# One layer's S5 in-chunk products moved ahead in the step order, their skewed table on two queues, output weights in whole rows

## The chip, the cores and the metric

The kernel runs on one core of a Trainium2 chip. The core has five engines that run side by side, each with an instruction stream of its own: TensorE (PE, matrix products; PEld is its weight load), VectorE (DVE), ScalarE (ACT), GpSimd (POOL) and SyncE (SP), which here only issues transfers. Transfers run on 16 DMA engines. The metric is the device time of one execution in microseconds (us). The kernel before took 1331.38 us, the median of three runs (1319.96 to 1343.16).

## The reference

256 latent tokens and 256 context tokens of width 1024 go through two layers in float32. Layer 0 has mLSTM heads beside attention. Layer 1, which the change touches, has S5 channels beside Mamba-2 (SSD) heads, and only its latent tokens are wanted at the end. Each layer closes with a mixture of 16 experts (MoE). Layer 1's mixer, cut to what matters:

```python
u_l, z_l, xbc_l, dt_l = split(h @ w_in)                       # and the same of the context
s5l = s5_output(s5_bidir(u_c, u_l, s5p), u_l, ...)            # gelu, then g * sigmoid(g @ glu_w + glu_b)
ssl = ssd_output(ssd_bidir(...), z_l, ssd_norm)               # y * silu(z), then an RMS norm
y = concatenate([s5l, ssl]) @ w_out                           # w_out is 1024 x 1024
```

`s5_bidir` runs a complex diagonal recurrence over the tokens in both directions for 32 groups of 16 channels and 64 states: `h = A h + B u`, `y = Re(C h)`. `ssd_bidir` is the chunked form of a scan over 8 heads: a term from within a chunk (`cb * decay`) and one from the state that is carried in.

## The kernel before, in words

**The whole.** Layer 0, its MoE, layer 1, its MoE stand one behind the other. The code is written in Python on a framework that orders the instructions of PE, DVE, ACT and POOL by a simulated schedule; the transfers on SP go out in the order of the code. `self.after(x, y)` only tells that scheduler to put x behind y, and sets no semaphore. What an engine waits for on the chip is set by data and by buffers alone.

**The stage of the change** is the second half of `layer1` (from L2131). It has four generators that give out work in steps, and the string `STEPS` (L1371) sets the order in which the loop at L2139 takes steps of them: S is the SSD heads, I the S5 in-chunk table, Y the S5 output products (C, the scan, was stepped before).

- **I, `s5_intra`** (L1587). For 32 groups it computes the response of a channel to another over 8 positions back and forth, a table E of 128 x 8 x 240, by 256 small matmuls (L1610, 32 columns of weights, 16 or 112 columns of data; those with `ca` or `v` among their operands read the S5 output tables). ACT copies the result out of PSUM (L1613), DVE adds the skip term (L1615), and POOL's queue writes E to a small DRAM table `ed` in 4 transfers (L1617).
- **The skew, `s5_skew`** (L1628). The table is read back from `ed` 8 times per half, each time shifted by 16, which makes the Toeplitz form: two tiles of 128 x 4 x 4 x 128, 1 MB each, called E and LL after the buffers they take. All 16 reads are on SP (L1633). The LL buffer holds SSD's decay products until then; E's buffer is a new one.
- **Y, `s5_y`** (L1736). In a pair of PSUM banks it sums five terms: n = 0 to 3 are the output tables times the scanned state `xs` (L1755), n = 4 is the skewed table times the input U. The last 16 products per half are those that read E and LL (L1755 with `E,U` and `LL,U`).
- **S, `ssd`**. State matmuls (L1996), decay products on DVE into LL (L2019), their products with x (L2022), the carried-state products (L2034), then a norm over DVE and ACT (L2041 to L2048) and 8 transposes (L2051) into `mix`.

Behind it come the gelu, its transposes and the GLU gate (L1767 to L1806), then `out_proj1` (L2160, called through `out_proj`): 2 token tiles x 4 column chunks of 256 x 8 row blocks of w_out. `out_w1` (L2145) loads w_out by column chunks into four buffers called `v`, on SP, behind the skew: each tile is one column chunk for all eight row blocks. Rows of w_out that belong to S5 go in a permuted order, by eight 16-partition transfers a tile.

The MoE of layer 1 streams three 2 MB weights per expert on SP (L941), and its products are L981, L1288 and L1302.

Of the kernel before, what the change touches and what calls it, by code (L numbers as in the profile page):

```python
# [21 lines left out]
D = 1024  # L22
KD = 8
# [1344 lines left out]
PI = math.pi  # L1368
SEGS = 32
SCAN = 4  # L1370
STEPS = "ISIIISSSIISIIIYSYSYYSYYYYYY"  # L1371


class Odd(Moe):
# [212 lines left out]
    def s5_intra(self, tb):  # L1587


        nc, a = self.nc, self.a  # L1590
        E = self.t("E", [128, 8, 240])
        (dk, idq), sk = self.dk, self.t("sk", [128, 8, 16])
        nc.vector.tensor_mul(sk, dk[:, :, None].to_broadcast([128, 8, 16]), idq[:, None, :].to_broadcast([128, 8, 16]))
        for x in range(4):
            p = [self.ps([128, 240], "ps") for _ in range(2)]
            for part in range(2):

                for z, d, r in [(0, 0, 0), (0, 0, 1), (0, 1, 0), (0, 1, 1), (1, 0, 0), (1, 0, 1)] if part == 0 else [(1, 1, 0), (1, 1, 1)]:
                    for q in range(4):
                        for gp in range(2):  # L1600
                            h, gh = slice(gp * 64, gp * 64 + 64), 4 * x + q
                            o, b = p[gp][32 * q:32 * q + 32], ((r * 2 + d) * 16 + gh) * 16

                            if z == 0:
                                o, rhs = o[:, 112:128], self.ct[h, r, d, gh, :]
                            elif d == 0:
                                o, rhs = o[:, 128:240], tb[0][r][h, gh, 0:7, :]
                            else:
                                o, rhs = o[:, 0:112], tb[1][r][h, gh, 0:7, :][:, ::-1, :]
                            self.lastI = nc.tensor.matmul(o, self.bf[h, b:b + 32], rhs, start=(r == 0 and (d == 0 or z == 1)), stop=(r == 1 and (d == 1 or z == 1)))  # L1610
                if part:
                    for gp in range(2):
                        nc.scalar.copy(E[:, gp * 4 + x, :], p[gp])  # L1613
                yield
        nc.vector.tensor_add(E[:, :, 112:128], E[:, :, 112:128], sk)  # L1615
        for q in range(4):
            nc.gpsimd.dma_start(self.ed[:, :, q, :], E[32 * q:32 * q + 16])  # L1617
        tb.append(self.s5_skew())
        yield
# [8 lines left out]
    def s5_skew(self):  # L1628

        mt = [self.t(tag, [128, 4, 4, 128]) for tag in ("E", "LL")]  # L1630
        for g in range(2):
            for s in range(8):
                self.nc.sync.dma_start(mt[g][16 * s:16 * s + 16], self.ed[:, 4 * g:4 * g + 4, :, (7 - s) * 16:(7 - s) * 16 + 128])  # L1633
        return mt


# [99 lines left out]
    def s5_y(self, U, xs, tb):  # L1736


        nc = self.nc
        pg = self.pg = [self.ps(tag="a") for _ in range(2)]  # L1740
        for n in range(5):
            for x in range(4):
                for gp in range(2):
                    h = slice(gp * 64, gp * 64 + 64)
                    for q in range(4):
                        gh = 4 * x + q
                        if n == 4:
                            lhs, rhs = U[:, 16 * gp + gh, 32:64], tb[2][gp][:, x, q, :]
                        else:
                            d, r = divmod(n, 2)  # L1750
                            k0 = 0 if d else SEGS - 1
                            lhs, rhs = xs[h, d, r, k0:k0 + SEGS, gh], tb[d][r][h, gh]
                            if d:
                                rhs = rhs[:, ::-1, :]
                        self.lastY = nc.tensor.matmul(pg[gp][32 * q:32 * q + 32, x * 128:(x + 1) * 128], lhs, rhs,  # L1755
                                                      start=(n == 0 and x == 0), stop=(n == 4 and x == 3))
                        self.after(self.lastY, self.lastI)
                if x % 2:
                    yield

    def s5_gelu(self):

        nc, pg = self.nc, self.pg
        g2 = self.t("xsT", [128, 2, 1024])
        gl = g2[:, 0].rearrange("p (t g x c) -> p t g x c", t=8, g=2, x=4)
        for gp in range(2):
            nc.scalar.activation(gl[:, :, gp].rearrange("p t x c -> p x t c"), pg[gp].rearrange("p (x t c) -> p x t c", x=4, t=8),  # L1767
                                 AF.Gelu_apprx_tanh)
        gT = g2[:, 1].rearrange("p (q t k) -> p q t k", q=4, t=8)
        for hf in range(2):  # L1770
            p = self.ps(tag="b")
            for t in range(4):
                nc.tensor.transpose(p[:, t * 128:(t + 1) * 128], gl[:, 4 * hf + t].rearrange("p g x c -> p (g x c)"), self.ident)
            o = gT[:, :, 4 * hf:4 * hf + 4, :].rearrange("p q t k -> p t q k")
            i = p.rearrange("p (t q k) -> p t q k", t=4, q=4)
            if hf:
                nc.scalar.copy(o, i)
            else:
                nc.vector.tensor_copy(o, i)
        return gT  # L1780
# [315 lines left out]
    def layer1(self):  # L2096
        nc = self.nc
        with self.phase("O", dict(ps=3, a=2, b=2, o=1), s2=5, s4=2, nz=1, scr=1, acsb=1, m8="nz"), \
# [34 lines left out]
            with self.sub("OC", ca=2, wp=1, E=1, sk="s2"):  # L2133
# [4 lines left out]
                steps = dict(S=self.ssd(R, mixS), I=self.s5_intra(tb), Y=self.s5_y(U, xs, tb), C=scan)  # L2138
                for step in STEPS:  # L2139
                    next(steps[step], None)  # L2140
# [4 lines left out]
    def out_w1(self):  # L2145

        nc, wo = self.nc, self.a["od_w_out"][0]
        ws = []
        for c in range(4):
            w, f = self.t("v", [128, KD, 256]), slice(256 * c, 256 * c + 256)  # L2150
            for x in range(8):
                self.after(nc.sync.dma_start(w[16 * x:16 * x + 16, 0:4], wo[64 * x:64 * x + 64, f].rearrange("(q c) f -> c q f", q=4)), self.lastS)
            nc.sync.dma_start(w[:, 4:8], wo[512:1024, f].rearrange("(k p) f -> p k f", p=128))
            ws.append(w)
        return ws

    def out_proj1(self, mix, ws):
        def mm(p, i, c4):
            for k in range(KD):
                o = self.nc.tensor.matmul(p, mix[k // 4][:, k % 4, i * 128 - 256:i * 128 - 128], ws[c4][:, k, :], start=(k == 0), stop=(k == KD - 1))  # L2160
            return o
        self.out_proj(mm, 1, (2, 3), (self.lastY,))

# [38 lines left out]
```

## Time and profile before

| what | value |
|---|---|
| median of three runs | 1331.38 us |
| profiled execution | 1328.82 us |
| its span, first to last instruction | 1327.2 us |
| mean granted TensorE clock | 0.927 |
| PE busy | 1137.6 us (86%) |
| DVE busy | 605.8 us (46%) |
| ACT busy | 304.1 us (23%) |
| POOL busy | 130.0 us (10%) |
| DMA | 330.40 MB, 249 GB/s over the span |
| the stage of the change, first in-chunk matmul to first of out_proj1 | 940.4 to 1016.8 us |

Times in rows are us from the start of the span. Busy times count work, not waits. The span is cut for the rows below by stretches of the stage, since a share over the whole span mixes stages with different limits. A float32 matmul leaves two records on PE. A row of waits says which engine stood, at which line, and what it waited for last.

### The profile page before, as it was taken

Reading aid. Unit: us, or ns where it says so; the run is one execution under the profiler, and the core shown is the slowest. Engines: PE = TensorE matmul, PEld = TensorE weight load, DVE = VectorE, ACT = ScalarE, POOL = GpSimd, SP = SyncE. Lnnn points to the kernel's source line nnn. Section 1 sums busy time; section 2 is a strip of 40 time slices with the busy share of each in tenths; the row PEclk is TensorE's granted clock in tenths of the full one; section 3 lists DMA queues with packets and bytes.
Section 4 is the critical chain, followed back from the end, with each engine's and each line's share of the span. In section 5 each row is a group of like instructions: output and inputs, shape, how many; then the busy total and the mean of one; then the engine's idle time right before and its main releaser. Section 6 shows DMA issues by size and latency. Waiting matters only on the chain. (4 is left out here: it accounts for less than half of the span.)

```text
span 1327.2 us, 23457 instructions
## 1 busy us (share of the span) xinstructions
PE 1137.6 (86%) x9689; PEld 701.2 (53%) x9689; DVE 605.8 (46%) x1647; ACT 304.1 (23%) x590; POOL 130.0 (10%) x185
## 2 busy tenths in 40 slices
PE   3899998977879599999999966967867789999895
PEld 0575564656579345545665525846756643432221
DVE  2657664186247521837013188799631531211112
ACT  2425441034121111111121134346221211110000
POOL 2002020000300251212101100000000000000000
PEclk8999999999989699999999986988767889999998
DMA  7876136703993899999999742342769859999960
GB/s 275 281 269 237 50 129 223 252 2 120 320 289 123 277 309 363 348 388 352 367 337 335 280 160 66 112 112 61 289 88 199 360 203 412 420 420 420 420 256 34
DMA packets 103973, 330.40 MB, mean 249 GB/s; under 512 B 18049, under 2 KB 56089, under 8 KB 78256
## 3 DMA queue, kind: packets, MB, share of 16 engines
q1 hardware_dynamic: 94592, 298.98, 63.2%
q0 software_dynamic: 9264, 29.81, 7.1%
q8 instruction: 80, 1.31, 0.4%
q14 instruction: 37, 0.30, 0.1%
HBM read 312.68 MB, written 18.01 MB: 249 GB/s over the span
## 5 line engine op out<-in xcount | busy, mean ns | idle before, releaser
L981 PE MATMUL ps<-wa,xT 128*32 128x512 f32 x848 | 167.2, 599 | 0.0
L981 PE MATMUL ps<-wb,xT 128*32 128x512 f32 x608 | 139.3, 594 | 0.0
L87 PE MATMUL ps<-wh,hT 128*128 128x256 f32 (+2 forms) x320 | 93.9, 294 | 6.5 <-ACT wh L381 4.7
L89 PE MATMUL ps<-wh,hT 128*128 128x256 f32 (+2 forms) x320 | 93.1, 293 | 4.0 <-DVE hT L315 4.0
L153 PE MATMUL ps<-w,cT 128*32 128x512 f32 x384 | 67.7, 782 | 28.2 <-DMA w<-in_ada_w_dram 24.2
L88 PE MATMUL ps<-wl,hT 128*128 128x256 f32 (+2 forms) x288 | 83.3, 290 | 1.4 <-DVE wl L383 1.4
L984 PE MATMUL ps<-wa,xT 128*32 128x256 f32 x496 | 82.9, 381 | 0.0
L984 PE MATMUL ps<-wb,xT 128*32 128x256 f32 x480 | 82.3, 380 | 0.0
L989 ACT ACTIVATE s<-ps 64x512 f32<-64x512 f32 (+1 forms) x48 | 23.4, 516 | 247.1 <-PE ps L981 246.6
L87 PE MATMUL ps<-hT,wh 128*128 128x512 f32 (+1 forms) x160 | 61.6, 385 | 14.4 <-DVE xs L1722 11.5
L87 PEld LDWEIGHTS ps<-wh,hT 128*128 128x128 f32 x320 | 62.6, 196 | 15.2 <-issue 6.1
L89 PEld LDWEIGHTS ps<-wh,hT 128*128 128x128 f32 x320 | 62.3, 196 | 15.5 <-issue 8.5
L981 PEld LDWEIGHTS ps<-wa,xT 128*32 128x32 f32 x848 | 45.0, 110 | 37.9 <-issue 24.7
L88 PE MATMUL ps<-hT,wh 128*128 128x512 f32 (+1 forms) x160 | 60.6, 379 | 0.0
L89 PE MATMUL ps<-hT,wl 128*128 128x512 f32 (+1 forms) x160 | 60.2, 377 | 0.2 <-DVE wl L1643 0.2
L88 PEld LDWEIGHTS ps<-wl,hT 128*128 128x128 f32 x288 | 55.2, 192 | 7.8 <-issue 5.9
L970 DVE COPY xT<-ps 128x384 f32<-128x384 f32 x16 | 8.9, 556 | 105.9 <-PE ps L984 98.3
L981 PEld LDWEIGHTS ps<-wb,xT 128*32 128x32 f32 x608 | 38.6, 110 | 21.8 <-issue 7.7
L1027 POOL DMA_INDIRECT yd<-y,si x30 | 34.5, 1149 | 155.6 <-ACT y L1018 150.2
L1275 DVE COPY aT<-ps 128x256 f32<-128x256 f32 x16 | 6.8, 424 | 89.3 <-PE ps L1273 89.3
L981 PE MATMUL ps<-wc,xT 128*32 128x512 f32 x288 | 46.5, 595 | 0.0
L87 PEld LDWEIGHTS ps<-hT,wh 128*128 128x128 f32 x160 | 31.8, 199 | 23.5 <-issue 15.7
(659 smaller groups left out, 2387.9 us busy)
## 6 DMA issues: line engine op xcount, KB each, us to landing
w<-in_ada_w_dram SPq DMA_DIRECT2D x96, 512.0 KB
wa<-in_moe_w_down_dram SPq DMA_DIRECT2D x30, 1024.0 KB
wa<-in_moe_w_up_dram SPq DMA_DIRECT2D x28, 1024.0 KB
wa<-in_moe_w_gate_dram SPq DMA_DIRECT2D x25, 1024.0 KB
wb<-in_moe_w_gate_dram SPq DMA_DIRECT2D x21, 1024.0 KB
wb<-in_moe_w_down_dram SPq DMA_DIRECT2D x17, 1024.0 KB
wb<-in_moe_w_up_dram SPq DMA_DIRECT2D x16, 1024.0 KB
w<-in_ev_w_in_dram SPq DMA_DIRECT2D x16, 512.0 KB
```

Of the source, the lines that this page charges most:

```text
L87: mm(p, x[0], y[0], start=first, stop=False)
L88: mm(p, x[0], y[1], start=False, stop=False)
L89: return mm(p, x[1], y[0], start=False, stop=last)
L153: o, i = nc.tensor.matmul(p[32 * q:32 * q + 32, :], self.cT[:, k, :], rhs, start=(k == 0), stop=(k == KD - 1)), o
L970: nc.vector.tensor_copy(xT[:, 0:4, :], p)
L981: self.up = nc.tensor.matmul(P[32 * j:32 * j + 32, :], xT[:, k, 32 * (j % 2):32 * (j % 2) + 32], (wg, wu)[j // 2](k), start=(k == 0), stop ...
L984: nc.tensor.matmul(Q[32 * j:32 * j + 32, :], xT[:, k, 64:96], (wg, wu)[j // 2](k)[:, (j % 2) * 256:(j % 2) * 256 + 256], start=(k == 0), s ...
L989: nc.scalar.activation(s, p[0:64, :], AF.Silu)
L1027: st = self.nc.gpsimd.indirect_dma_start(out=rows, out_offset=bass.IndirectOffsetOnAxis(ap=idx, axis=0), in_=y, in_offset=None, bounds_che ...
L1275: nc.vector.tensor_copy(aT, tr)
```

## The change

The order of the steps is changed: all steps of I now stand in front of Y and of all but two steps of S (five of S stood among them), and the last of S comes at the end. `s5_intra` goes through its two parts outermost and the four x inside, so that it holds four PSUM banks instead of two at a time, and copies two x at once. The skew's second half is issued on POOL's queue. `s5_y` takes all of E before all of LL in its last term. `out_w1` cuts w_out by rows: four tiles of 256 whole rows (4 KB each), two of them in eight 128 KB transfers and two in one of 1 MB, held behind the last in-chunk matmul in the scheduler's order; `out_proj1` then reads row block k from tile k // 2.

```diff
--- before.py
+++ after.py
@@ -1368,7 +1368,7 @@
 PI = math.pi
 SEGS = 32
 SCAN = 4
-STEPS = "ISIIISSSIISIIIYSYSYYSYYYYYY"
+STEPS = "IISISIIIIIISYSYSYSYYSYYYYYS"
 
 
 class Odd(Moe):
@@ -1591,10 +1591,11 @@
         E = self.t("E", [128, 8, 240])
         (dk, idq), sk = self.dk, self.t("sk", [128, 8, 16])
         nc.vector.tensor_mul(sk, dk[:, :, None].to_broadcast([128, 8, 16]), idq[:, None, :].to_broadcast([128, 8, 16]))
-        for x in range(4):
-            p = [self.ps([128, 240], "ps") for _ in range(2)]
-            for part in range(2):
-
+        P = [[self.ps([128, 2, 240], tag) for _ in range(2)] for tag in ("ps", "a")]
+
+        for part in range(2):
+            for x in range(4):
+                p = [t[:, x % 2] for t in P[x // 2]]
                 for z, d, r in [(0, 0, 0), (0, 0, 1), (0, 1, 0), (0, 1, 1), (1, 0, 0), (1, 0, 1)] if part == 0 else [(1, 1, 0), (1, 1, 1)]:
                     for q in range(4):
                         for gp in range(2):
@@ -1608,9 +1609,9 @@
                             else:
                                 o, rhs = o[:, 0:112], tb[1][r][h, gh, 0:7, :][:, ::-1, :]
                             self.lastI = nc.tensor.matmul(o, self.bf[h, b:b + 32], rhs, start=(r == 0 and (d == 0 or z == 1)), stop=(r == 1 and (d == 1 or z == 1)))
-                if part:
+                if part and x % 2:
                     for gp in range(2):
-                        nc.scalar.copy(E[:, gp * 4 + x, :], p[gp])
+                        nc.scalar.copy(E[:, gp * 4 + x - 1:gp * 4 + x + 1, :], P[x // 2][gp])
                 yield
         nc.vector.tensor_add(E[:, :, 112:128], E[:, :, 112:128], sk)
         for q in range(4):
@@ -1628,9 +1629,9 @@
     def s5_skew(self):
 
         mt = [self.t(tag, [128, 4, 4, 128]) for tag in ("E", "LL")]
-        for g in range(2):
+        for g, eng in enumerate((self.nc.sync, self.nc.gpsimd)):
             for s in range(8):
-                self.nc.sync.dma_start(mt[g][16 * s:16 * s + 16], self.ed[:, 4 * g:4 * g + 4, :, (7 - s) * 16:(7 - s) * 16 + 128])
+                eng.dma_start(mt[g][16 * s:16 * s + 16], self.ed[:, 4 * g:4 * g + 4, :, (7 - s) * 16:(7 - s) * 16 + 128])
         return mt
 
 
@@ -1739,24 +1740,28 @@
         nc = self.nc
         pg = self.pg = [self.ps(tag="a") for _ in range(2)]
         for n in range(5):
-            for x in range(4):
-                for gp in range(2):
-                    h = slice(gp * 64, gp * 64 + 64)
-                    for q in range(4):
-                        gh = 4 * x + q
-                        if n == 4:
-                            lhs, rhs = U[:, 16 * gp + gh, 32:64], tb[2][gp][:, x, q, :]
-                        else:
-                            d, r = divmod(n, 2)
-                            k0 = 0 if d else SEGS - 1
-                            lhs, rhs = xs[h, d, r, k0:k0 + SEGS, gh], tb[d][r][h, gh]
-                            if d:
-                                rhs = rhs[:, ::-1, :]
-                        self.lastY = nc.tensor.matmul(pg[gp][32 * q:32 * q + 32, x * 128:(x + 1) * 128], lhs, rhs,
-                                                      start=(n == 0 and x == 0), stop=(n == 4 and x == 3))
-                        self.after(self.lastY, self.lastI)
-                if x % 2:
+            hold = [self.lastI]
+            for j in range(8):
+                x, gp = divmod(j, 2) if n < 4 else (j % 4, j // 4)
+                h = slice(gp * 64, gp * 64 + 64)
+                for q in range(4):
+                    gh = 4 * x + q
+                    if n == 4:
+                        lhs, rhs = U[:, 16 * gp + gh, 32:64], tb[2][gp][:, x, q, :]
+                    else:
+                        d, r = divmod(n, 2)
+                        k0 = 0 if d else SEGS - 1
+                        lhs, rhs = xs[h, d, r, k0:k0 + SEGS, gh], tb[d][r][h, gh]
+                        if d:
+                            rhs = rhs[:, ::-1, :]
+                    self.lastY = nc.tensor.matmul(pg[gp][32 * q:32 * q + 32, x * 128:(x + 1) * 128], lhs, rhs,
+                                                  start=(n == 0 and x == 0), stop=(n == 4 and x == 3))
+                    self.after(self.lastY, *hold)
+                if j == 3:
+                    if n == 4:
+                        hold = [self.lastY]
                     yield
+            yield
 
     def s5_gelu(self):
 
@@ -2145,19 +2150,21 @@
     def out_w1(self):
 
         nc, wo = self.nc, self.a["od_w_out"][0]
-        ws = []
-        for c in range(4):
-            w, f = self.t("v", [128, KD, 256]), slice(256 * c, 256 * c + 256)
-            for x in range(8):
-                self.after(nc.sync.dma_start(w[16 * x:16 * x + 16, 0:4], wo[64 * x:64 * x + 64, f].rearrange("(q c) f -> c q f", q=4)), self.lastS)
-            nc.sync.dma_start(w[:, 4:8], wo[512:1024, f].rearrange("(k p) f -> p k f", p=128))
-            ws.append(w)
+        ws = [self.t("v", [128, 2, D]) for _ in range(4)]
+        for j, w in enumerate(ws):
+            if j > 1:
+                self.after(nc.sync.dma_start(w, wo[256 * j:256 * j + 256, :].rearrange("(k p) f -> p k f", p=128)), self.lastI)
+            else:
+                for x in range(8):
+                    c = 64 * x + 32 * j
+                    self.after(nc.sync.dma_start(w[16 * x:16 * x + 16], wo[c:c + 32, :].rearrange("(q c) f -> c q f", q=2)), self.lastI)
         return ws
 
     def out_proj1(self, mix, ws):
         def mm(p, i, c4):
             for k in range(KD):
-                o = self.nc.tensor.matmul(p, mix[k // 4][:, k % 4, i * 128 - 256:i * 128 - 128], ws[c4][:, k, :], start=(k == 0), stop=(k == KD - 1))
+                o = self.nc.tensor.matmul(p, mix[k // 4][:, k % 4, i * 128 - 256:i * 128 - 128],
+                                          ws[k // 2][:, k % 2, 256 * c4:256 * c4 + 256], start=(k == 0), stop=(k == KD - 1))
             return o
         self.out_proj(mm, 1, (2, 3), (self.lastY,))
```

Three places show what that does to the order. On PE, ahead of the S5 output products; `ps` is PSUM, `ca` and `v` are output tables, `bc` the input tables, `xs` the scanned state, `xsT` SSD states, `LL` the decay products. Before, the last in-chunk products with output and carried-state products behind them, all other SSD products being ahead:

```order
L1610 MATMUL ps_9896<-ca_9561,bc_4866 32x112
L1610 MATMUL ps_9897<-ca_9561,bc_4866 32x112
L1755 MATMUL ps_9987<-v_9551,xs_8307 32x128 x4
L1755 MATMUL ps_9988<-v_9551,xs_8307 32x128 x4
...
L2034 MATMUL ps_10005<-xsT_9650,v_9223 128x256 x2
L2034 MATMUL ps_10011<-xsT_9650,v_9223 128x256 x2
```

And now:

```order
L1611 MATMUL ps_9602<-ca_9561,bc_4866 32x112
L1611 MATMUL ps_9603<-ca_9561,bc_4866 32x112
L2020 MATMUL ps_9933<-v_9223 128x128 x2
L2020 MATMUL ps_9968<-v_9223 128x128
L1757 MATMUL ps_9950<-v_9551,xs_8307 32x128 x5
L1757 MATMUL ps_9951<-v_9551,xs_8307 32x128
L2027 MATMUL ps_9938<-v_9044,LL_9389 128x64 x4
L1757 MATMUL ps_9951<-v_9551,xs_8307 32x128 x3
...
```

The last in-chunk products have moved ahead of the decay products' matmuls (L2027), which stood 100 rows ahead of them before, as half of the carried-state products did (L2034). On DVE, around the add to E (L1615, now L1616); `s` are work tiles. Before:

```order
L2019 TENSOR_TENSOR LL_9389<-LL_9389,ps_9799 128x512 x2
L2026 TENSOR_TENSOR s_1678_9796<-s_1678_9796,ps_9787 128x512
L2026 TENSOR_TENSOR s_1681_9813<-s_1681_9813,ps_9804 128x512
L2036 TENSOR_TENSOR s_1685_9887<-ps_9884,ea_8714 128x512
L2038 TENSOR_TENSOR s_1678_9796<-s_1678_9796,s_1685_9887 128x512
...
L2041 TENSOR_TENSOR s_1678_9796<-s_1678_9796,nz_9300 128x512
L1615 TENSOR_TENSOR E_9597<-E_9597,s_1653_9598 128x8x16
```

And now:

```order
L2029 TENSOR_TENSOR s_1685_9982<-v_9044,sdk_8297 128x512
L2024 TENSOR_TENSOR LL_9389<-LL_9389,ps_9933 128x512
L1616 TENSOR_TENSOR E_9597<-E_9597,s_1653_9598 128x8x16
L2024 TENSOR_TENSOR LL_9389<-LL_9389,ps_9933 128x512
L2031 TENSOR_TENSOR s_1680_9947<-s_1680_9947,ps_9938 128x512
L2024 TENSOR_TENSOR LL_9389<-LL_9389,ps_9968 128x512 x2
L2031 TENSOR_TENSOR s_1685_9982<-s_1685_9982,ps_9973 128x512
```

The add now stands behind the first of the four multiplies into LL, ahead of all that follows. On SP, the transfers before:

```order
L1793 DMA s_1650_9585<-in_s_glu_w_dram 16x2x512 x8
L1633 DMA E_9969<-ed 16x16x128 x8
L1633 DMA LL_9970<-ed 16x16x128 x8
L2152 DMA v_10204<-in_od_w_out_dram 16x4x256 x8
L2153 DMA v_10204<-in_od_w_out_dram 128x4x256
...
L785 DMA rw_10294<-in_moe_gr_w_dram 128x8x4
```

Now, first on SP and, in the second fence, on POOL:

```order
L1798 DMA s_1650_9585<-in_s_glu_w_dram 16x2x512 x8
L1634 DMA E_9914<-ed 16x16x128 x8
L2160 DMA v_10196<-in_od_w_out_dram 16x2x1024 x8
L2160 DMA v_10197<-in_od_w_out_dram 16x2x1024 x8
L2156 DMA v_10198<-in_od_w_out_dram 128x2x1024
L2156 DMA v_10199<-in_od_w_out_dram 128x2x1024
L785 DMA rw_10268<-in_moe_gr_w_dram 128x8x4
```

```order
L941 DMA wc_10560<-in_moe_w_up_dram 128x2048
L1318 IOTA tok_10579 128x2
L1618 DMA ed<-E_9597 128x1x240 x4
L1634 DMA LL_9915<-ed 16x16x128 x8
L234 DMA s_1723_10265<-mod_2826 128x1024
```

The reads into LL have left SP for POOL's queue, behind the writes of the table, and the output weights follow the reads into E.

## Rows read from the trace of the kernel before

**Rows 1.** Windows: busy us and instructions per engine, granted TensorE clock, DMA.

```profile
core 0: us, PE busy (x) PEld busy (x) DVE busy (x) ACT busy (x) POOL busy (x), PEclk, DMA share, GB/s
947.00:970.00 23.00, 22.45 (x274) 18.39 (x274) 10.21 (x19) 2.72 (x8) 0.00 (x0) 0.50 0.53 192
984.00:1003.00 19.00, 4.14 (x88) 2.96 (x90) 0.00 (x0) 3.67 (x6) 0.00 (x0) 0.50 1.23 123
1003.00:1022.00 19.00, 17.62 (x96) 14.51 (x89) 3.88 (x7) 4.76 (x9) 0.34 (x1) 0.77 0.87 203
```

**Rows 2.** Waits of 936 to 1060: us in total, times, the longest.

```profile
PE ps L1755 <- DMA LL<-ed: 8.1, 1, 8.1
...
PE ps L1755 <- DMA v<-in_od_w_out_dram: 6.7, 1, 6.7
```

**Rows 3.** Timeline of PE: start, us, instructions, idle before.

```profile
982.46 0.45 PE L2051 MATMUL ps<-ident,s 128*128 128x128 f32 x1 [4.14 <-DVE s L2048]
...
993.99 0.60 PE L1755 MATMUL ps<-E,U 128*32 128x128 f32 x5 [8.12 <-DMA LL<-ed]
...
1002.66 0.44 PE L1755 MATMUL ps<-LL,U 128*32 128x128 f32 x4 [6.74 <-DMA v<-in_od_w_out_dram]
...
1004.12 0.47 PE L1755 MATMUL ps<-LL,U 128*32 128x128 f32 x4
...
1016.77 0.38 PE L2160 MATMUL ps<-v,acsb 128*128 128x256 f32 x1
```

**Rows 4.** Timeline of DVE, POOL and SP: E's add, write, reads; loads around them.

```profile
974.12 0.28 DVE L1615 TENSOR_TENSOR E<-E,s 128x128 f32<-128x128 f32 x1
...
974.70 2.15 POOL L1617 DMA_DIRECT2D ed<-E  x4 [33.17 <-DVE E L1615]
...
950.64 13.44 SPq L1793 DMA_DIRECT2D s<-in_s_glu_w_dram  x16
...
981.62 5.49 SPq L1633 DMA_DIRECT2D E<-ed  x8
```

**Rows 5.** Timeline of PE; windows of L1610, L1996 (two each), L2022, L2034 alone.

```profile
940.37 0.70 PE L1610 MATMUL ps<-bc 64*32 64x16 f32 x61
...
947.55 0.39 PE L1610 MATMUL ps<-ca,bc 64*32 64x112 f32 x2 [2.89 <-issue]
...
966.40:968.60 2.20, 2.20 (x112) 1.88 (x112) 0.50 0.04 7
...
971.60:973.10 1.50, 1.50 (x128) 1.30 (x128) 1.00 0.00 0
...
941.50:943.40 1.90, 1.90 (x8) 1.43 (x8) 1.00 0.98 336
948.00:950.90 2.90, 2.84 (x6) 1.85 (x6) 0.50 1.02 418
...
958.90:964.10 5.20, 5.16 (x24) 5.13 (x24) 0.50 0.36 111
...
973.60:975.50 1.90, 1.90 (x8) 1.39 (x8) 1.00 0.00 0
```

**Rows 6.** Timeline of DVE: the scan's last operation; the multiplies into LL.

```profile
948.62 0.22 DVE L1722 TENSOR_TENSOR xs<-xs,sct 128x64 f32<-128x64 f32 x1
...
958.03 2.48 DVE L2019 TENSOR_TENSOR LL<-LL,ps 128x512 f32<-128x512 f32 x4 [0.16 <-PE ps L2015]
```

**Rows 7.** Window with a POOL queue's broadcast beside SP's 512-byte rows; columns of rows 1.

```profile
874.00:878.00 4.00, 2.77 (x13) 1.95 (x11) 4.00 (x10) 1.04 (x1) 0.24 (x1) 1.00 0.96 251
```

**Rows 8.** MoE of layer 1: a window, the stream's restart on SP, waits of 1072 to 1320.

```profile
1080.00:1282.00 202.00, 193.88 (x1546) 69.35 (x1542) 34.55 (x63) 20.72 (x33) 0.00 (x0) 1.00 1.01 416
...
1077.36 0.33 SPq L941 DMA_DIRECT2D wc<-in_moe_w_gate_dram  x1
...
PE ps L1302 <- ACT yh L1291: 7.3, 9, 0.8
...
PE ps L1288 <- DVE aT L1275: 4.1, 8, 0.5
```

## The prediction

> **What bounds the kernel now.** I read the page's engine table first and distrusted it: PE is busy 86% of the span, but the change touches one stage of some 75 us, and what counts is which wait ends last there. So the windows of that stage came next [rows 1]. In 947.00:970.00 PE works almost without a pause, but at a granted clock of 0.50 (the 1.2 GHz level; just before, in [rows 5], it is 1.00, 2.4 GHz); in 984.00:1003.00 it has 4.14 us of work in 19. That last stretch is the stall. The waits [rows 2] name it: PE stands 8.1 us for the table E and 6.7 us more for its second half LL. The releaser of the second is written as the output weights, but the rows on the queue show that LL's own load is what ends. The timeline [rows 3] gives the edges: the SSD transposes (L2051) begin at 982.46, the E products at 993.99 and the LL products at 1002.66, the last of which ends at 1004.12 + 0.47 = 1004.59; out_proj1 starts 12.2 later, at 1016.77. Before the transposes PE idles 4.14 for the SSD norm, which is short of the table's wait: two paths run side by side, and the table's is the longer by some 20 us.
>
> The table's path, followed back [rows 4]: the last in-chunk matmul ends at 973.10 [rows 5], the add to E at 974.40, POOL writes E to DRAM with issues that end at 976.85, and SP, which waits for that write, issues the skewed reads at 981.62. So 7.2 us lie between add and skew. E may be used 993.99 - 981.62 = 12.4 after the skew starts, both halves 1002.66 - 981.62 = 21.0 after it: 2 MB at about 100 GB/s, in a window that moved 123 GB/s for everything.
>
> **The change, step by step.** *The order of the steps.* The order on PE shows that the in-chunk matmuls (L1610, now L1611) no longer end behind SSD's decay products (L2022) and half of its carried-state products; they are ahead of both. Their price (a matmul is two records): 128 records in 1.50 us at full clock, 11.7 ns each, and 112 in 2.20 at half clock, 19.6 each [rows 5]. All 512 cost 6.0 or 10.1. The 20 records of SSD state matmuls still among them cost 8 in 1.90 at full clock, 6 in 2.84 at half [rows 5]: 4.8 or 9.4. PE's 2.89 us of idle at 947.55 stays, for its operands come off DVE: the scan holds DVE until 948.62 + 0.22 = 948.84 [rows 6]. I leave 2 us more for DVE to make the later state operands. From 940.4, where the first in-chunk matmuls stand [rows 5], full clock gives 940.4 + 6.0 + 4.8 + 2.9 + 2 = 956. At half clock from 947 on, about three quarters of the work pays double; by the same sum that is 961 to 964, and I take 961 since DVE then has time to run ahead. Last in-chunk matmul: 956 to 961, against 973.10.
>
> *The copies out of PSUM* become four of twice the width. Two remain behind the last matmul. The add comes 1.3 after the last matmul in the trace (974.40 - 973.10); I allow up to 2, since on DVE one long multiply now stands close ahead of it (each about 0.62, from four in 2.48 [rows 6]). Add done: 957.5 to 963. With the 7.2 us of write and landing unchanged, the skew starts at 965 to 970, 12 to 17 earlier. SP's issue of the glu weights, ahead of it on that queue, ends at 950.64 + 13.44 = 964.08 [rows 4] and just does not hold it.
>
> *The skew on two queues.* E goes out on SP as before. LL goes out on POOL's queue, with nothing but one iota and a load of the modulation behind it. But LL's tile is SSD's decay table, and the load may not begin before the last product that reads it (L2022, now L2027). Ahead of that stand DVE's 2.5 us of multiplies [rows 6] and 32 records, 24 of which take 5.16 at half clock [rows 5] (6.9 for all, about 3.5 at full). So LL is free at 956 + 2.5 + 3.5 + 1 = 963, or 961 + 2.5 + 6.9 + 1.6 = 972. What two queues of such short packets do together the trace does not show in this place. One bound is no gain: 21.0 for both, whatever the queues. The other is that each half takes its own 12.4. Nearest is 874.00:878.00, where a POOL queue and SP's together moved 251 GB/s [rows 7], twice the skew's 123; so I take the overlap: both landed at 976 to 984. In series it is 986 to 991. That the halves are slower together than in turn no row suggests.
>
> The Trainium skill speaks against this edit ("DMA: Bandwidth & Descriptors", "Rules for kernel authors"): spreading DMAs over several issuing engines does not raise bandwidth, since all run on the same 16 DMA engines; only issue time is saved. By it both halves would still take their 21.0, and the sum would be rival C's; in its favour stands the share of 1.23 in the last window of [rows 1].
>
> *The SSD path* is now close to the table's. Behind the last LL read come its carried-state products (L2034, now L2039), 16 records, 8 in 1.90 at full clock [rows 5], so 3.8, and 7.6 at half, part of it done while DVE multiplies: they end at 967 to 978. From the end of the last of them (975.50 [rows 5]) to the transposes at 982.46 the trace has 7.0 us of DVE and ACT work for the norm, and this stays: transposes at 974 to 985, done 1.2 to 1.9 later. Then E and LL products, 1.93 each (1002.66 to 1004.59), 3.9 in all.
>
> The end of the LL products is thus the later of two paths. The table gives at most 984 + 1.9 = 986, the SSD path 979 to 991. I take 987, where full clock is lost for part of the stretch: 1004.6 - 987 = 17.6, **17 us** earlier.
>
> *The output weights in whole rows*: 18 loads instead of 36, with 4 KB runs instead of 1 KB. But the first chunk of out_proj1 now reads all four tiles where it read one. They are needed at 1016.8 - 17 = 1000. The tiles come free early (the S5 state, C and the S5 output tables), and the loads queue on SP behind E's skew only, from 984 at worst. 4.2 MB need 20.7 us at the 203 GB/s of 1003.00:1022.00 [rows 1], which gives 1004.7; at the 251 GB/s of [rows 7], 16.7, which gives 1000.7. Runs of 4 KB are longer than those of either stage, so I take the second or better and cost the step at nothing; its cover is the 12.2 us between the products and out_proj1, and the bad end is +5.
>
> *The clock behind the stall.* In 1003.00:1022.00 the clock is 0.77 on average [rows 1]: PE comes out of its stall at half clock, and (1 - 0.77) / 0.5 = 46% of the 19 us, 8.7 us, are spent so. At full clock that work would take 4.4 less. The gelu between leaves pauses of its own, so I take **2 us**, with 0 and 4 as ends.
>
> *MoE of layer 1.* It runs on PE, with the weight stream at 416 GB/s and a share of 1.01 from 1080.00 to 1282.00 [rows 8]. The stream restarts at 1077.36, when the first expert frees its tile, so it moves earlier with PE, and the shift carries through. Some experts wait 0.5 on DVE (4.1 in eight places) and then 0.8 on ACT (7.3 in nine) [rows 8]; the changed order on PE has one expert fewer in that arrangement, 4.1/8 + 7.3/9 = 1.3, of which I take **1 us**.
>
> Sum: 17 + 2 + 1 = 20 off the profiled execution of 1328.8, 1308.8. The median of the three runs is 1331.4, 2.6 above it, so 1311 on that scale; I predict **1310**.
>
> **The rivals.** *A, the forecast*: 1309, between 1300 and 1317 (at the top the weights 5 late and nothing for the clock behind the stall; at the bottom products 6 earlier, since both paths have ends near 980, and the clock term at 4).
>
> *B, full clock all through.* PE falls to 0.50 behind its idle of 2.89 [rows 5]. If matmuls packed earlier keep it at the 2.4 GHz level, the first case of every sum holds: products end near 980, gain 24.5 + 3 = 27, 1302. For it: ten more microseconds of work now stand ahead of the idle. Against: the idle is due to DVE and the order up to there is nearly unchanged.
>
> *C, the skew goes no faster on two queues.* Its 21.0 stay and start at 965 to 970; products end at 988 to 994, gain 10.6 + 3, 1315. For it: both halves read one small DRAM table in short pieces, and the share of the window is already over 1. Against: 251 GB/s in [rows 7].
>
> *D, given back later.* The MoE stream is full at 1.01, and if its loads rather than PE set the end of the last expert, an earlier start of PE only lengthens waits: 1325 to 1329. Against: the stream's own restart hangs on PE.
>
> *E, slower.* The output weights arrive late. Everything else gained is then lost, since out_proj1 can't start its first chunk without the last tile. The point from which it decides is a landing after 1016.8. At the skew's 123 GB/s 4.2 MB take 34 us; started at 990, beside LL's load, they land at 1024, 7 late: 1336. For it: the old first chunk needed 1 MB only. Against: 203 GB/s with shorter runs.
>
> That the change does not do what it says is no rival left: the order has the in-chunk products ahead, and both queues.
>
> **How the numbers follow.** Chances: A 46%, B 20%, C 18%, D 9%, E 4%, and 3% for something else. The first three all lie between 1295 and 1320 with their own spread. The range runs from 1294 (B with its clock term at 4 is 1300, and 6 more for the spread of runs, of which the three shown span 23) to 1328 (C with the weights 5 late, and most of D); E, the top of D and the bottom of B are left out, under 2 in 10. About what can be told from no change is 2%, 26.6 us: below 1304.8 is faster, above 1358 slower. Faster: two thirds of B and a fifth of A, 0.23. Slower: a bad form of E only, 0.02. The rest, 0.75, is within 2%, nearly all of it on the faster side.
>
> **What would show it.** The E add at 958 to 963 (were 974.4) tests the order; the skew's first read at 965 to 970 the write behind it; E and LL products within 2 us of the transposes tests the two queues, and a second wait of 5 or more for LL would mean C. The granted clock of 947 to 970 separates A from B. out_proj1 should start near 1000; if its wait names the output weights, the step "cost at nothing" failed. If out_proj1 starts 17 early but the end moves by under 5, it is D. What would make the prediction wrong altogether is a new wait on DVE or POOL ahead of the add, which I have only by the order, not by a duration.

## The result, and the profile after

The changed kernel took 1318.47 us (median of 20 runs, 1312.57 to 1326.96), the kernel before 1329.09 in as many (1319.71 to 1347.52): ratio 0.9935, 95% interval 0.9913 to 0.9956, some 9 us faster. The ratio is one of means and leaves out two slow executions of the kernel before (1343.16 and 1347.52), so it is nearer to 1 than the medians' 0.992. A gain of 20 us was forecast. The time lies in the forecast range of 1294 to 1328, but the gain does not come near the forecast one.

In the profiled execution after, the stage begins 8.5 us later than before (the first in-chunk matmul at 948.90 instead of 940.37). No instruction ahead of it was changed, the profiled execution is the longest of the twenty (1326.96), and in the profiles of the fifteen experiments this start lies between 940.7 and 951.3. So the table counts from the first in-chunk matmul.

| us from the first in-chunk matmul | before | forecast | after | order alone (first experiment) |
|---|---|---|---|---|
| add to E done | 34.0 | 17 to 22.6 | 21.6 | 21.5 |
| first read of the skew | 41.2 | 24.6 to 29.6 | 28.3 | 28.9 |
| SSD transposes begin | 42.1 | 34 to 45 | 39.6 | 39.5 |
| E products begin | 53.6 | about 43 | 52.3 | 41.4 |
| LL products end | 64.2 | 46.6 | 55.9 | 50.2 |
| out_proj1 begins | 76.4 | about 59 | 68.8 | 62.4 |
| end of the span | 386.8 | 367 | 376.4 | 372.7 |

Everything up to the transposes came as forecast. Then PE waits for the skewed table. The timeline of PE after, against [rows 3, 5]:

```profile
956.23 0.95 PE L1611 MATMUL ps<-v,bc 64*32 64x112 f32 x19 [5.37 <-issue]
...
988.53 1.94 PE L2056 MATMUL ps<-ident,s 128*128 128x128 f32 x8 [1.51 <-DVE s L2053]
...
1001.15 1.93 PE L1757 MATMUL ps<-E,U 128*32 128x128 f32 x32 [10.69 <-DMA v<-in_od_w_out_dram]
...
1002.83 1.96 PE L1757 MATMUL ps<-LL,U 128*32 128x128 f32 x32
...
1017.74 1.46 PE L2166 MATMUL ps<-v,acsb 128*128 128x256 f32 x6
```

One wait of 10.69 stands where two of 8.12 and 6.74 were; it is named after the output weights, but E is what the products read. DVE's add, POOL's write and the transfers of POOL and SP, against [rows 4]:

```profile
970.17 0.28 DVE L1616 TENSOR_TENSOR E<-E,s 128x128 f32<-128x128 f32 x1
...
970.75 2.15 POOL L1618 DMA_DIRECT2D ed<-E  x4 [20.69 <-DVE E L1616]
977.83 2.79 POOL L1634 DMA_DIRECT2D LL<-ed  x5 [4.93 <-DVE s L2031]
982.10 1.67 POOL L1634 DMA_DIRECT2D LL<-ed  x3 [1.48 <-issue]
983.93 0.58 POOL L234 DMA_DIRECT2D s<-mod  x1 [0.16 <-issue]
...
977.23 3.85 SPq L1634 DMA_DIRECT2D E<-ed  x8
981.19 26.55 SPq L2160 DMA_DIRECT2D v<-in_od_w_out_dram  x16
```

Both halves go out at once, within 6.5 us. But E can be used 1001.15 - 977.23 = 23.9 us after the first read, where it took 12.4 before and both halves took 21.0. What each queue moved from 978 to 997 (packets, MB, the time of its packets as a share of the 16 engines' span; q0 is POOL's queue, q1 is SP's), and behind it the same for the window of [rows 7] in the kernel before:

```profile
q0 software_dynamic: 416, 1.18, 58.2%
q1 hardware_dynamic: 2059, 1.00, 52.7%
...
q0 software_dynamic: 250, 1.00, 96.0%
```

SP's queue moved 1.00 MB in that time, less than E's own 1.05 MB. So the output weights, which stand behind E on that queue, had hardly begun (in the packets of the trace, their first starts at 997.4, and E's last ends at 999.7). What travels beside E is on POOL's queue: LL, and a 512 KB broadcast of the gate (L234). The two queues share the engines about evenly. E, LL and the broadcast are 2.62 MB, which at the 123 GB/s of [rows 1] take 21.3 us; they took 21.5, from 978.2 to 999.7. So E is late because all three finish together, and not because the rate fell. The last line says that [rows 7] was misread: in 874.00:878.00 everything moved on POOL's queue, and nothing on SP's.

The windows after, against [rows 1]:

```profile
core 0: us, PE busy (x) PEld busy (x) DVE busy (x) ACT busy (x) POOL busy (x), PEclk, DMA share, GB/s
956.00:962.00 6.00, 5.77 (x117) 4.24 (x122) 2.74 (x5) 0.00 (x0) 0.00 (x0) 0.50 1.00 387
962.00:969.00 7.00, 6.60 (x259) 5.10 (x244) 4.83 (x8) 1.49 (x3) 0.00 (x0) 0.99 0.64 203
986.00:990.00 4.00, 2.49 (x39) 2.07 (x40) 2.73 (x11) 0.35 (x1) 0.00 (x0) 0.51 1.23 125
990.00:1001.00 11.00, 0.47 (x3) 0.07 (x1) 0.00 (x0) 3.14 (x5) 0.00 (x0) 0.50 1.08 149
```

With two queues the DMA engines move 125 GB/s at a share of 1.23, as with one: [rows 1] has 123 at 1.23. (The share adds up the time of all packets; it passes 1 when an engine has several under way.) The 149 of the last window takes in the start of the weights. The granted clock is half for some 6 us behind PE's pause of 5.37, and full again from 962 on, where it was half for 23 us. MoE's waits of 1064 to the end, against [rows 8]:

```profile
PE ps L1302 <- ACT yh L1291: 6.5, 8, 0.8
...
PE ps L1288 <- DVE aT L1275: 3.6, 7, 0.5
```

One expert fewer waits, as the order said.

### The profile page after: what moved, and what is told of

It is laid out like the page before. It is cut to its first block, busy times and chain, and to the rows that moved or that the text cites. A ratio compares the mean times of both kernels' runs of the same rounds, so it can differ in the third digit from the quotient of the medians.

```text
span 1325.3 us, 23433 instructions
## 1 busy us (share of the span) xinstructions
PE 1138.0 (86%) x9689; PEld 696.1 (53%) x9689; DVE 606.2 (46%) x1647; ACT 304.0 (23%) x586; POOL 134.1 (10%) x193
## 3 DMA queue, kind: packets, MB, share of 16 engines
q1 hardware_dynamic: 89056, 297.93, 62.4%
```

## The experiments

All runs are edits of the changed kernel; a run "on one queue" puts LL's reads back on SP. "E" and "LL" are the us from the skew's first read to the first product that reads the half, in the profiled execution of each run; differences under 1 to 2 us there are not resolved. In the changed kernel they are 23.9 and 25.6. Ratios are to the kernel before, with the 95% interval; products, out_proj1 and the end of the span count from the first in-chunk matmul. The expectations name theories: P, the 16-partition form of the transfers is the limit; Q, their short pieces are; W and W2, the output weights take part of the rate; M, the gate's broadcast does; P2, two queues are slower together than one.

**1. The order alone.** One queue, and `out_w1` and `out_proj1` as before.

> The step order and the two halves alone: both halves of the skew on SP, the output weights in column chunks as before. In the changed kernel E and LL could be used 23.9 us after the skew's first read, against 12.4 (E) and 21.0 (LL) before. If two queues bring nothing (theory P, the 16-partition writes are the limit, and theory Q, the short pieces are), E products start 12 to 13 and LL products 20 to 22 after the first read, the products end 2 to 4 us earlier than in the changed kernel, and the time is at or below its 0.9935 of before: 0.990 to 0.994. If the two queues did help, LL is 26 or more behind and the ratio is 0.996 to 0.999.

E 12.5, LL 19.3, ratio 0.9908 (0.9870 to 0.9945). The queues and the whole rows bring nothing on top of the order; in the profile they cost 3.7 us at the end of the span, which the ratios do not resolve.

```profile
976.39 5.13 SPq L1634 DMA_DIRECT2D E<-ed  x8
981.63 6.67 SPq L1634 DMA_DIRECT2D LL<-ed  x8
...
971.61 0.57 POOL L234 DMA_DIRECT2D s<-mod  x1 [0.20 <-issue]
...
988.91 1.94 PE L1757 MATMUL ps<-E,U 128*32 128x128 f32 x32
995.73 1.93 PE L1757 MATMUL ps<-LL,U 128*32 128x128 f32 x32 [4.88 <-DMA v<-in_od_w_out_dram]
```

With E first and alone, its products follow the transposes without a wait. The broadcast has left POOL 5 us ahead of the skew.

**2. The queues at different partitions.** `for s in ((0, 1, 2, 3, 4, 5, 6, 7), (4, 5, 6, 7, 0, 1, 2, 3))[g]:` in `s5_skew`.

> The changed kernel with one edit: the second half is read in the order s = 4..7, 0..3, so that the two queues write to different 16-partition groups at any time. Theory P (a 16-partition transfer fills only an eighth of the partitions, and two queues that walk them in step meet at the same ones): the rate in the skew rises from about 115 to 160 to 220 GB/s and the products start 11 to 17 us after the first read instead of 23.9; ratio to before 0.984 to 0.989. Theory Q (512-byte pieces of one small DRAM table, or the engines being full): 23 to 25 us as in the changed kernel, ratio 0.992 to 0.995.

E 22.6, LL 24.3, ratio 0.9923 (0.9890 to 0.9957), the rate in the skew unchanged:

```profile
980.00:984.00 4.00, 1.37 (x14) 1.32 (x7) 2.88 (x12) 0.16 (x1) 0.00 (x0) 0.50 1.18 120
```

That the two queues meet at the same partitions is not it.

**3. The weights on POOL's queue.** `nc.sync` becomes `nc.gpsimd` in `out_w1`.

> The changed kernel with the 18 loads of the output weights on POOL's queue, behind LL's reads, instead of on SP behind E's. If the weights' loads in the middle of the skew are what cost it (theory W), the products start 17 to 19 us after the first read instead of 23.9, as 2 MB at 116 GB/s give. Under P and Q the sum of bytes ahead is the same once LL is done, so 20 to 22. The weights then land later; out_proj1 may wait for them, up to 10 us behind the GLU. Ratio 0.990 to 1.000.

E 23.9, LL 25.6, ratio 0.9991 (0.9962 to 1.0019). No help for the table. But one of the 128 KB loads left ahead of LL (969.56) and the others followed LL on POOL's queue, so they travelled beside E in the place of the broadcast, which left at 1004.27 only; the run tells little of W. What settles W is the queue rows above: in the changed kernel the weights on SP hardly move before E is in. out_proj1 began at 73.1 (68.8 changed).

**4. The skew to all partitions.**

```diff
-            for s in range(8):
-                eng.dma_start(mt[g][16 * s:16 * s + 16], self.ed[...])   # cut
+            for i in range(16):
+                src = bass.AP(t.tensor, t.offset + (16 * g + i) * 240, [[16, 8], [7680, 16], [1, 128]])
+                eng.dma_start(mt[g][:, i // 4, i % 4, :], src)
```

(`t` is the view of the whole table; the edits that store it in reverse and read it so are left out here.)

> The changed kernel with each half of the skew read by 16 transfers to all 128 partitions (64 KB each) instead of 8 transfers to 16 partitions (128 KB each); the pieces stay 512 bytes. The table is stored with its positions reversed for it, which costs no instruction. Theory P: the rate doubles at least (200 GB/s and more), the products start within 13 us of the first read instead of 23.9, ratio 0.982 to 0.988. Theory Q: the same 4096 pieces at the same rate, 22 us or more, ratio 0.992 or above.

Ratio 0.9879 (0.9833 to 0.9926). Windows, the first inside the skew, the second when the weights had come in; behind them PE's waits for the table:

```profile
982.00:986.00 4.00, 2.44 (x160) 2.20 (x144) 3.14 (x6) 1.46 (x4) 3.54 (x7) 1.00 0.71 183
...
990.00:994.00 4.00, 2.90 (x31) 2.05 (x29) 0.00 (x0) 3.12 (x5) 0.59 (x1) 0.50 1.10 137
...
PE ps L1759 <- DMA E<-ed: 3.4, 3, 1.9
PE ps L1759 <- DMA LL<-ed: 1.2, 1, 1.2
```

The same 512-byte pieces go at 183 GB/s and a share of 0.71: by byte, 2.5 times less DMA time (1.23 / 125 against 0.71 / 183). So the form of the transfers is the limit, not the pieces. E's products could begin right behind the transposes, 13.5 after the first read, but the last of E's sixteen reads kept them up to LL's 20.2: three of the four waits are for E.

**5. Two queues, old weights** (undo of `out_w1` and `out_proj1` alone).

> The new step order and LL on POOL's queue, but the output weights in column chunks as before. With the order alone E could be used 12.5 us after the skew's first read and LL 19.3; in the changed kernel both only after 24 to 25.6. If the two queues do that (theory P: both halves share the 100 to 130 GB/s of 16-partition transfers, so that E lands no earlier than LL), E comes 21 to 25 us after the first read here too, and the ratio is 0.992 to 0.996. If the weights in whole rows do it (theory W), E comes 12 to 15 after and LL 18 to 20, ratio 0.989 to 0.992.

E 23.0, LL 24.7, ratio 0.9968 (0.9938 to 0.9997): the second queue makes E late, not the whole rows.

**6. One queue, whole rows** (`self.nc.gpsimd` back to `self.nc.sync` alone).

> The other corner: the new step order and the output weights in whole rows, but both halves of the skew on SP. Theory P: E 12 to 13 us after the first read, LL 19 to 21, ratio 0.988 to 0.992, as with the order alone (0.9908). Theory W: the whole rows hold up out_proj1 or the table as in the changed kernel; out_proj1 starts 66 us or more after the first in-chunk matmul (62.4 with the order alone, 68.8 changed), ratio 0.993 to 0.996.

E 13.2, LL 21.4, ratio 0.9925 (0.9898 to 0.9952). With 1 and 5 this makes a square: LL's products end at 50.2 (order alone), 55.0 (with the queues), 52.5 (with the rows), 55.9 (with both). The intervals of the four ratios overlap, so the square rests on one profile each.

**7 and 8. Weights to all partitions as well**, on two queues and on one. On top of 4, the S5 rows by `[[64 * D, 8], [D, 16], [1, D]]`, four loads of 512 KB.

> The changed kernel with both halves of the skew and the S5 rows of the output weights in transfers to all 128 partitions (16 of 64 KB per half, and 4 of 512 KB in place of 16 of 128 KB). With the skew alone so, the rate was 183 to 196 GB/s until the weights' 16-partition loads came, and fell to 137 behind them; LL could be used 20.2 us after the first read. Theory P: without those, LL comes 12 to 15 after the first read, the products end 44 to 47 us after the first in-chunk matmul (56.0 changed, 51.9 with the skew alone), out_proj1 starts at 57 to 60, ratio 0.981 to 0.986. Theory Q (short pieces): LL at 19 to 21 again, ratio 0.987 to 0.990.

> As the run before, with both halves on SP, E first. 32 issues of some 0.4 to 0.5 us on one queue: E at 8 to 12 after the first read (hidden by the transposes at 11), LL at 15 to 18. If a second queue saves issue time and nothing else, this is 2 to 4 us behind the run before; if E's being first matters more, it is level. Ratio 0.982 to 0.988.

Ratios 0.9946 (0.9921 to 0.9971) and 0.9988 (0.9955 to 1.0021): misses. The products end at 47.8 and 52.8, so 8 us are gained in 7, but out_proj1 takes 40.2 us from its first to its last matmul instead of 33.4, and the span ends at 375.1 (376.4 changed). In 8 one queue of 64 KB transfers moves only 109 GB/s at a share of 0.44, and SP's 32 issues fill 20.5 us back to back. So here issuing is the limit, and the second queue is worth 5 us.

**9. The weights held back.** `nc.sync.dma_start(self.dr.tile([128, 1], ...), tb[2][1][:, 0, 0, 0:1])` ahead of them.

> The changed kernel with the output weights kept out of the skew: a store of one column of LL to DRAM stands ahead of their loads on SP, so that they can't be issued before LL has landed. (One store more, nothing left out.) Theory W2 (the weights, which pass LL on SP now that LL has left that queue, take their share of the 100 to 130 GB/s): products 18 to 20.5 us after the first read instead of 24.0. Theory P2 (two queues of 16-partition transfers are slower together than one): still 22 to 25. The weights start later by some 12 us in either case and out_proj1 may wait for them: ratio 0.990 to 1.000.

E 23.8, LL 25.5, ratio 0.9959 (0.9928 to 0.9990). The store, which waits for LL, left at 993.58, the products came later still, with E:

```profile
993.58 0.34 SPq L2154 DMA_DIRECT2D hold<-LL  x1
...
997.54 1.93 PE L1757 MATMUL ps<-E,U 128*32 128x128 f32 x32 [10.63 <-DMA v<-in_od_w_out_dram]
```

W2 falls: with the weights held back E is as late, as the queue rows above would have it.

**10 and 11. The router's loads ahead.** The four small loads of `moe_prep` move to before `s5_out(1, "ca")`; 10 is 7 with that, 11 has the skew of the order alone and the weights of 7.

> Both halves of the skew and the S5 rows of the output weights to all 128 partitions, as in the run of that kind on two queues, and the four loads of the router's weights and biases moved ahead on SP, to before the second pair of output tables, where SP waits for a buffer. In that run the products ended 8 us earlier than in the changed kernel, but out_proj1 took 40.3 us from its first to its last matmul instead of 33, with DVE waiting 4.6 us for the router's weights ahead of out_proj1's first addition. If that wait is what ate the gain, out_proj1 is back at 33 us, the end comes 7 us earlier than there, and the ratio is 0.983 to 0.988. If something else did (slow clock, the weights' own landing), out_proj1 stays at 37 or more and the ratio at 0.992 to 0.996.

> The new step order, both halves of the skew on SP in 16-partition transfers as before, and behind them the output weights in 128-partition transfers, the router's loads moved ahead as in the run before. E 12 to 13 us after the first read, LL 18 to 20 (the weights reach SP only at LL's end). Products end at 49 to 51 us after the first in-chunk matmul, as with the order alone (50.2), out_proj1 starts at 61 to 63. Ratio 0.987 to 0.992. If 128-partition loads beside LL cost as much as 16-partition ones, LL comes at 21 or more.

Ratios 0.9957 (0.9931 to 0.9984), the second branch of the expectation, and 0.9984 (0.9954 to 1.0014), a miss. The products of 11 end at 50.6 as forecast, those of 10 at 45.9, and out_proj1 of 10 begins at 55.4. DVE's wait for the router is gone, but out_proj1 now takes 46.0 us, for it waits for its weights (waits of PE in 10):

```profile
PE ps L2176 <- DMA v<-in_od_w_out_dram: 9.1, 5, 3.9
```

The theory that the router's wait had eaten the gain falls: the last matmul of out_proj1 starts at 101.0 in 7 and 101.4 in 10. In this form the weights are late, the cover of the forecast's "cost at nothing" being gone once the products end early. Why these loads are slow was not tried.

**12. The gate's broadcast first.** `self.gates[1, 1] = self.bcast(self.md[1], 1, 0)` ahead of `tb.append(self.s5_skew())`, nothing else.

> The changed kernel with one transfer moved: the broadcast of layer 1's gate (512 KB from the modulation table, POOL's queue) goes out ahead of LL's reads instead of behind them. In the changed kernel it left at 983.93, in the middle of the skew; with the order alone, where LL is not on POOL's queue, it left at 971.61, while SP waited for the table to be written. Theory M (this transfer, at the 116 GB/s of the stage 4.4 us, is what the second queue costs): products 19 to 21.5 us after the first read instead of 24.0, ratio 0.988 to 0.992. Theory P2 (two queues of 16-partition transfers are slower together): still 23 to 25, ratio 0.992 to 0.996.

E 19.6, LL 21.3, ratio 0.9895 (0.9840 to 0.9950). POOL and PE:

```profile
972.00 0.57 POOL L234 DMA_DIRECT2D s<-mod  x1 [0.18 <-issue]
976.94 2.81 POOL L1637 DMA_DIRECT2D LL<-ed  x5 [4.36 <-DVE s L2034]
...
995.61 1.93 PE L1760 MATMUL ps<-E,U 128*32 128x128 f32 x32 [6.24 <-DMA v<-in_od_w_out_dram]
```

The wait falls from 10.69 to 6.24, by the 4.4 that theory M gave for 512 KB. And LL at 21.3 is what one queue gives (21.4 in 6): for the second half, two queues are worth nothing and cost nothing, beside what they push into the skew. The first half pays: E 19.6, against 13.2 on one queue.

**13. The same with old weights.**

> The same move in the kernel with two queues and the output weights in column chunks (there: E 23.0, LL 24.7 after the first read; one queue: 12.5 and 19.3). Theory M: both halves 18 to 20.5 after the first read, end level with the order alone, ratio 0.989 to 0.993. Theory P2: E stays at 22 or more, ratio 0.994 to 0.998.

E 21.5, LL 23.1, ratio 0.9924 (0.9893 to 0.9955): only 1.6 better than 5, a miss for M's 18 to 20.5. The weights, which follow E on SP, are not what takes the rest: from 974 to 991 SP's queue moved 0.93 MB, less than E alone. The difference is at the edge of what the profiles resolve, and its cause stays open.

**14 and 15. Both out of the way**: 4 with the broadcast first, with whole rows (14) and with column chunks (15).

> The skew in 128-partition transfers on two queues (there: LL 20.2 after the first read, ratio 0.9879) with the gate's broadcast ahead of it. 2 MB at 185 to 200 GB/s are 11 us: LL 14 to 17, the products end 46 to 49 us after the first in-chunk matmul (51.9 there, 56.0 changed). The weights' 16-partition loads come in behind E's reads as before, so out_proj1 may start by the weights and not by the products: 60 to 65, ratio 0.984 to 0.989.

> As the run before with the output weights in column chunks, of which out_proj1's first chunk needs one tile only, and with the router's wait on DVE behind the fourth addition instead of ahead of the first. Products as there; if the late weights are what is left, out_proj1 starts 58 to 61 us after the first in-chunk matmul and the ratio is 0.982 to 0.987, the best of all; if the column chunks' short runs cost as much elsewhere, level with the run before.

14: LL 20.3, a miss (14 to 17), ratio 0.9886 (0.9842 to 0.9929). PE waits in it for E's last reads, and not for LL:

```profile
PE ps L1762 <- DMA E<-ed: 4.1, 4, 1.9
```

15: LL 15.2, the products end at 45.8 with no wait for the table, out_proj1 begins at 55.6, the span ends at 368.4, ratio 0.9908 (0.9871 to 0.9945), where 0.982 to 0.987 was expected. 14 and 15 differ in the output weights alone: in these two profiles whole rows behind E on SP held up E's last reads, and column chunks did not. Windows and PE of 15:

```profile
984.00:988.00 4.00, 2.94 (x161) 2.38 (x160) 3.49 (x6) 1.13 (x3) 3.45 (x7) 1.00 0.73 180
988.00:992.00 4.00, 0.00 (x0) 0.00 (x0) 3.20 (x15) 0.32 (x2) 3.00 (x6) 0.65 0.81 204
```

```profile
995.94 1.20 PE L1762 MATMUL ps<-LL,U 128*32 128x128 f32 x29
...
1006.97 5.33 PE L2170 MATMUL ps<-v,acsb 128*128 128x256 f32 x23
```

So the forecast's largest term is there with the table out of the way: 64.2 - 45.8 = 18.4 us, for 17. In the time it is not all seen: 0.9908 is 12 us, with 7 to 17 in the interval, against 18.4 in the profile. Runs 1, 4, 12, 14 and 15 lie level within their intervals; 4 (0.9879) and 14 have the lowest ratios, ahead of the changed kernel by about half a per cent, with intervals that touch its own.

## Why the prediction was wrong, step by step

- **The order of the steps: right.** The last in-chunk matmul starts 19.7 us after the first (15.6 to 20.6 forecast), the add and the first read lie inside their ranges. The pause ahead of the state products was 5.37, not 2.89, and the clock came back sooner than forecast.
- **The SSD path: right**, the transposes 39.6 after the start.
- **The skew on two queues: the step that failed.** "So I take the overlap: both landed at 976 to 984" gave each half its own 12.4 us; measured from the first read are 23.9 for E and 25.6 for LL. The step rests on 251 GB/s of another stage [rows 7], read as two queues together. It was POOL's queue alone (1.00 MB, none on SP's), and its transfers go to 128 partitions, where the skew's go to 16 each. Of that form one queue moved 114 to 133 GB/s in windows of 4 us, at a share over 1.2, and two moved 102 to 136. The row that should have been nearest was the skew itself, whose share of 1.23 in [rows 1] said that the engines were busy, not waiting for issues. The rule of the Trainium skill on issuing engines that the prediction cites ("DMA: Bandwidth & Descriptors", "Rules for kernel authors") holds in this case: LL at 21.3 us on two queues (run 12), 21.4 on one (run 6). I gave the case 18%.
- **Worse than rival C.** C kept the 21.0; it was 23.9 to 25.6. LL's reads on POOL push the gate's broadcast, which was ahead of the skew, into it (4.4 us, run 12), and E, which alone would have been hidden by the transposes (run 1), lands as late as LL. I had named that load as standing behind LL on POOL and given it no price. The sign I gave for C, a second wait of 5 or more for LL, did not come either: both halves were late together, in one wait of 10.69. That the time lies in the range is owed to its width, which was drawn to take in C.
- **The output weights: right as a sum in this kernel.** out_proj1 does not wait for them. Their cover is gone in runs 10 and 11.
- **The clock behind the stall, 2: wrong.** From the last LL product to out_proj1 it takes 12.9 instead of 12.2, at a mean granted clock of 0.67 instead of 0.71: PE still comes out of a wait of 10 us at half clock (0.50 in 990.00:1001.00). From out_proj1 to the MoE's selection (L869) 1.2 were gained.
- **MoE, 1:** 1.6 (262.4 to 260.8). D did not occur.

The sum by measured terms: 8.3 (the table's 17) - 0.7 + 1.2 (the clock's 2) + 1.6 (the MoE's 1) = 10.4 in the profile counted from the stage's start, for 17 + 2 + 1 = 20.

## What to carry to other kernels

Before a load is split over two queues, read the DMA share of its own window: where it was over 1 at a low rate, as here, the transfers' form was the limit, and the second queue only changed who goes first. Ask what the move lets past: here the half that was needed first lost its lead, and a transfer that had gone out early fell behind the moved one. And before the rate of another stage stands for yours, look at which queues moved its bytes, and whether its transfers cover as many partitions.

## What was not expected of the hardware

The skew's loads of 128 KB to 16 partitions ran at 102 to 136 GB/s in windows of 4 us, with the DMA engines' share at 1.07 to 1.29, in the kernels with them, and sending two queues to different groups of 16 changed nothing (120 at 1.18). The same pieces to 128 partitions, in loads of 64 KB, moved at 183 GB/s with a share of 0.71. By what the first form loses its time these runs do not show.
